# GpSimd subtractions and residual steps issued as four 256-column quarters, residual steps issued behind the first feed-forward products, and one engine per PSUM bank for scaling transposed blocks

## The chip, the cores and the metric

The kernel runs on one core of a Trainium2 chip. The metric is device time in microseconds (us). The engines are named as in the profile: PE is TensorE's matmul, PEld its weight load, DVE is VectorE, ACT is ScalarE, POOL is GpSimd, SP is SyncE, which here only issues transfers. SBUF is the memory on the chip that the engines work in, PSUM the eight banks that PE writes.

## The reference

Four residual layers of two blocks work on 256 tokens of width 1024, in float32. What matters here is the first block:

```python
for layer in range(2):                     # layer 0: latent attention, layer 1: state space mixer
    for mixer in (attention_or_ssm, mlp):
        scale, shift, gate = split(silu(c) @ W_mod + b_mod, 3)
        y = mixer(x * (1 + scale) + shift)         # mlp: relu(h @ W1)**2 @ W2
        x = layer_norm(ALPHA * x + (1 + gate) * y) # with a gain g and a bias b
```

The second block follows it: two layers with gated feed-forwards of hidden width 2816 before and behind a gated linear recurrence ("lru") in one layer and a block-sparse attention in the other, with RMS normalisation.

## The kernel before

The 256 tokens are two halves of 128 partitions. Weights come from HBM as units of 128x1024 float32 (512 KB) into seven raw buffers, in the order of a list. Each unit is split into two fp32r parts: `wh` is a copy made on ACT (L454), `wl = raw - wh` a subtraction (L455) on DVE for 445 units and on POOL for the 39 units of a table called POOLED. Every product is then made in three passes (xh·wh, xh·wl, xl·wh). Units of the modulation weights are not split but reduced on DVE (L504). A queue of the next units runs beside the products: each product step emits what is needed to prepare units further on, and each engine works its own instructions in that order.

A layer ends, and the next begins, in `boundary()`. The last products of tokens half 0 come first. Their result is gated and added to the old x (`ln_part`: L643, L644), its mean and variance are taken (L645 to L649, with one power on POOL, L627), and R is normalised in place by two DVE instructions of 128x512 (L658). Then `turn_x` (L593) transposes the eight 128x128 blocks of R[half] into two PSUM banks of four blocks each, a few units before the last products of the other half are through. `make_xt` scales each transposed block with a factor and a shift per feature, which are columns, and splits the result into xh (ACT, L585) and xl (DVE, L586). In one bank, blocks 0 and 2 are scaled on DVE (L610) and blocks 1 and 3 on ACT (L608). Three boundaries have this scaling: behind the attention's output (called mla_o, at 144 to 190 us), behind the first feed-forward (mlp0.d, 396 to 430 us) and behind the state space mixer (ssm_out, 555 to 596 us). With half 0 turned, the first product of the next layer for half 0 runs, then the same for half 1.

At the three boundaries POOL also makes the new residual for the next layer, x = r*g + b, for both halves in two instructions of 128x1024 each (`ln_resid`, L661 and L662). They are issued at the end of `boundary()`, and the next layer's `f_evac` copies the first products of a feed-forward layer out of PSUM into the same tiles R that the residual is made from.

Of the kernel before, what the change touches and what calls it, by code (L numbers as in the profile page):

```python
# [15 lines left out]
OP = mybir.AluOpType  # L16
# [36 lines left out]
# ------------------------------------------------------------ the order in which weights come  # L53
# [67 lines left out]
# ------------------------------------------------------------------------- host side layout  # L121
# [192 lines left out]
# ------------------------------------------------------------------------------- the kernel  # L314
class Model:
# [54 lines left out]
    # ---- small helpers  # L370
# [29 lines left out]
    # ---- weights  # L400
# [22 lines left out]
    def run(self, look=LOOK, maxn=99, mods=2):  # L423
        n = 0
        while self.nproc < len(UNITS) and n < maxn:
            i = self.nproc
            u = UNITS[i]
            if WPOS[i] > WPOS[self.ntake] + look:
                break
            if u[0] == "m":  # L430
                if mods == 0 or (self.hold and self.modfin is not None):
                    break
                mods -= 1
            self._issue(i + 1)
            if self.ndma <= i:
                break
            raw = self.raw[RPOS[i] % RAWN]
            self.settle(KEEP)
            if u[0] == "w":
                while self.rt and self.nw % RING in SPARE:  # L440
                    self.nw += 1
                s = self.nw % RING
                own = self.slot_owner[s]
                if own is not None and own not in self.finished:
                    break
                if own is None and s >= RING - 3 and self.early:
                    break
                if self.Hs[s] is None:
                    self.Hs[s], self.Ls[s] = (self.sb.tile([128, 1024], F32R, name="w%s%d_%d" % (c, s, i), tag="w%s%d" % (c, s))
                                              for c in "hl")  # L450
                self.nw += 1
                self.slot_owner[s] = u
                self.slot_of[u] = s
                self.nc.scalar.activation(self.Hs[s], raw, func=AF.Copy)  # L454
                (self.nc.gpsimd if u[1:] in POOLED else self.nc.vector).tensor_tensor(  # L455
                    self.Ls[s], raw, self.f32(self.Hs[s]), op=OP.subtract)
            elif u[0] == "m":
                self.mod_unit(u, raw)
# [29 lines left out]
    # ---- modulation: silu(c) @ w + b  # L488
# [44 lines left out]
    # ---- one step of the tensor engine has been emitted: t is its time in us  # L533
# [16 lines left out]
    # ---- matrix products in three float32r passes  # L550
# [37 lines left out]
    # ---- token-major -> feature-major, with a factor (and a shift) per feature  # L588
# [7 lines left out]
    def xt_evac(self, b, half, g, f, s, sh, perm):  # L596
        nc = self.nc
        hs = slice(128 * half, 128 * half + 128)
        ks = slice(4 * g, 4 * g + 4)
        f3 = (b if s is None else f).rearrange("p (k t) -> p k t", k=4)  # L600
        if s is not None:
            for j in range(4):
                k = 4 * g + j
                o, i = f[:, 128 * j:128 * j + 128], b[:, 128 * j:128 * j + 128]
                if perm:
                    o, i = o.rearrange("p (j k) -> p k j", j=4), i.rearrange("p (k j) -> p k j", j=4)
                if j % 2:
                    nc.scalar.activation(o, i, func=AF.Identity, scale=s[:, k:k + 1], bias=sh[:, k:k + 1])  # L608
                else:
                    nc.vector.tensor_scalar(o, i, s[:, k:k + 1], sh[:, k:k + 1], op0=OP.mult, op1=OP.add)  # L610
        self.split(self.XH[:, ks, hs], self.XL[:, ks, hs], f3)
        self.rel(b)
# [4 lines left out]
    def make_xt(self, half, bs, s=None, sh=None, perm=False):  # L617
        for g in range(2):
            self.xt_evac(bs[g], half, g, self.Z[2][:, 512 * (2 * half + g):512 * (2 * half + g) + 512], s, sh, perm)

    # ---- normalisations, one half of the tokens at a time
# [38 lines left out]
    def ln_resid(self, half, eng):  # L660
        eng.tensor_tensor(self.X[half], self.R[half], self.GR, op=OP.mult)  # L661
        eng.tensor_tensor(self.X[half], self.X[half], self.BR, op=OP.add)  # L662

    # x / rms(x) * pre, from the sums of squares
# [33 lines left out]
    # ---- the end of one layer and the start of the next  # L698
# [66 lines left out]
    # ---- feed-forward layers  # L765
    def ffn(self, tag, nt, first, begin, b1=None, epi=None, mid=None):
# [8 lines left out]
        for m in range(first, nt, 2):  # L775
# [12 lines left out]
            if m == first:  # L788
                self.f_hidden(pair, b1)
                if tag == "mlp0":  # L790
                    self.bg, self.hold = self.ssm_operators(), True
                if accs is None:
                    accs = [[self.bank(), self.bank()] for h in range(2)]
# [29 lines left out]
    def f_evac(self, half, outs, pair):  # L823
        nc, R = self.nc, self.R[half]
# [19 lines left out]
    def f_hidden(self, pair, b1):  # L844
        for i in range(2 if pair else 4):
            b = self.pair_transposes(self.R, 2 * i)
# [25 lines left out]
    # ---- small accurate functions on narrow tiles  # L872
# [36 lines left out]
    # ---- start: constants, rotary tables, first modulation  # L909
# [84 lines left out]
    # ---- attention of one head over 256 tokens, causal  # L994
# [29 lines left out]
    # ---- latent attention  # L1024
    def mla(self):
# [121 lines left out]
        def norm(h):  # L1147
            if h == 1:
# [6 lines left out]
                             self.post_ln, "mlp0.f", kouter=True, gate="mod02")  # L1155
# [5 lines left out]
    # one head after another, its stages spread over the next ones (a digit is the lag in heads)  # L1161
# [54 lines left out]
    # ---- state space layer: operators from the parameters  # L1216
# [97 lines left out]
    # tables of rotations and rows of the input operators (powers times B)  # L1314
# [42 lines left out]
    def ssm_operators(self):  # L1357
# [7 lines left out]
        # output operators, and the part within a chunk  # L1365
# [116 lines left out]
    # ---- state space layer: 64 chunks of 4 tokens, two groups of channels at a time  # L1482
    def ssm(self, begin):
# [154 lines left out]
        for i in range(4):  # L1638
            t = self.Z[2][:, 512 * i:512 * i + 512]
            for j in range(2):  # L1640
# [15 lines left out]
                             self.post_ln, "mlp1.f", kouter=True, gate="mod22")  # L1656
# [17 lines left out]
    # ---- gated linear recurrence  # L1674
# [27 lines left out]
    def lru(self, begin):  # L1702
# [4 lines left out]
        self.f_evac(0, fa, False)  # L1707
        fb = self.f_pass(1, fu)
        self.f_evac(1, fb, False)
# [124 lines left out]
    # ---- keys and values, kept over one feed-forward layer  # L1834
# [25 lines left out]
    def moba(self, begin):  # L1860
        nc = self.nc
        fu, fa = begin
        self.f_evac(0, fa, False)
        fb = self.f_pass(1, fu)
        self.f_evac(1, fb, False)
# [26 lines left out]
    # ---- the whole  # L1892
# [113 lines left out]
```

## Time and profile before

| | |
|---|---|
| three runs | 1795.33, 1793.89, 1794.28 us, median 1794.28 |
| span of the profiled execution | 1790.9 us (its time outside the span is not listed; the median is 3.4 us above the span) |
| busy shares | PE 90%, PEld 79%, DVE 67%, ACT 47%, POOL 24% |
| mean granted TensorE clock | 0.95 of full speed |
| DMA | 349.6 MB, mean 195 GB/s |

PE is the busiest engine by far. What it doesn't work, some 180 us, is spread over many places, and each such place has its own wait. A busy share tells nothing of them; the list of PE's waits by releaser and the timeline around each place do.

### The profile page before, as it was taken

The page shows a single profiled execution, that of the slowest core. Times are in us where ns is not written, and L with a number is a line of the kernel's source. Part 1 is how long each engine was busy: PE and PEld are TensorE (multiplying, and loading weights), DVE is VectorE, ACT ScalarE, POOL GpSimd, SP SyncE. Part 2 cuts the span into 40 slices and gives each one's busy share as a digit, 9 for nine tenths or more (in the row PEclk, how much of TensorE's full clock was granted, in tenths as well). Part 3 has the DMA queues.
Part 4 walks back from the last instruction along what each step waited for, and adds up shares of the span by engine and source line. Part 5 has one row for each costly group of instructions (what it writes and reads, how often), then busy time and mean ns, then how long its engine had stood idle before and what let it go on. Part 6 is the DMA issues. An engine that isn't in the chain of part 4 may idle for free. (4 is left out here: it accounts for less than half of the span.)

```text
span 1790.9 us, 25130 instructions
## 1 busy us (share of the span) xinstructions
PE 1607.8 (90%) x9690; PEld 1417.8 (79%) x9690; DVE 1192.7 (67%) x1480; ACT 835.3 (47%) x1252; POOL 433.7 (24%) x404
## 2 busy tenths in 40 slices
PE   4777998898778999999999838999999999899998
PEld 2555798786676799879998827999899999779997
DVE  6688795567988755586556787555656554856553
ACT  2342645565334645444445545444445444744441
POOL 8943198714725200000002351000000001120000
PEclk9869999898798999999999969999999999999999
DMA  9476577775655466645553433656356564526640
GB/s 370 165 267 215 203 262 261 252 270 192 224 184 200 174 247 220 229 170 205 196 172 127 134 126 133 230 204 204 113 212 220 179 225 142 177 95 223 207 158 24
DMA packets 106587, 349.63 MB, mean 195 GB/s; under 512 B 12385, under 2 KB 22753, under 8 KB 106466
## 3 DMA queue, kind: packets, MB, share of 16 engines
q1 hardware_dynamic: 106466, 348.02, 55.3%
q8 instruction: 76, 1.25, 0.3%
q14 instruction: 45, 0.37, 0.1%
HBM read 338.40 MB, written 9.57 MB: 194 GB/s over the span
## 5 line engine op out<-in xcount | busy, mean ns | idle before, releaser
L455 DVE TENSOR_TENSOR wl<-raw,wh 128x1024 fp32r<-128x1024 f32 x445 | 567.9, 1310 | 191.2 <-ACT wh L454 188.9
L454 ACT ACTIVATE wh<-raw 128x1024 fp32r<-128x1024 f32 x484 | 490.1, 1051 | 268.6 <-PE bank L392 135.0
L392 PE MATMUL bank<-xh,wh 128*128 128x256 f32 x1728 | 490.4, 284 | 0.0
L392 PE MATMUL bank<-xh,wl 128*128 128x256 f32 x1728 | 489.6, 283 | 0.0
L392 PE MATMUL bank<-xl,wh 128*128 128x256 f32 x1728 | 489.1, 283 | 0.0
L392 PEld LDWEIGHTS bank<-xh,wh 128*128 128x128 f32 x1728 | 331.1, 192 | 2.6 <-DVE z L1560 0.2
L392 PEld LDWEIGHTS bank<-xl,wh 128*128 128x128 f32 x1728 | 331.0, 192 | 2.1
L392 PEld LDWEIGHTS bank<-xh,wl 128*128 128x128 f32 x1728 | 330.9, 191 | 0.0
L392 PE MATMUL bank<-wh,hh 128*128 128x512 f32 x736 | 294.9, 401 | 30.8 <-ACT hh L1812 27.1
L392 PE MATMUL bank<-wl,hh 128*128 128x512 f32 x736 | 292.1, 397 | 2.6 <-POOL wl L455 2.5
L392 PE MATMUL bank<-wh,hl 128*128 128x512 f32 x736 | 243.3, 396 | 6.8 <-DVE hl L586 4.9
L627 POOL TENSOR_TENSOR st<-st,mhalf 128x1 f32<-128x1 f32 (+1 forms) x33 | 21.9, 664 | 720.1 <-DVE st L635 623.7
L392 PEld LDWEIGHTS bank<-wh,hh 128*128 128x128 f32 x736 | 140.7, 191 | 62.3 <-ACT hh L1812 28.4
L392 PEld LDWEIGHTS bank<-wh,hl 128*128 128x128 f32 x736 | 139.9, 190 | 40.1 <-DVE hl L586 5.7
L392 PEld LDWEIGHTS bank<-wl,hh 128*128 128x128 f32 x736 | 140.8, 191 | 32.2 <-POOL wl L455 3.7
L455 POOL TENSOR_TENSOR wl<-raw,wh 128x1024 fp32r<-128x1024 f32 x39 | 106.5, 2745 | 184.1 <-ACT wh L454 183.4
L504 DVE SCALAR_TENSOR_TENSOR junk<-raw,cs 128x1024 bf16<-128x1024 f32 x96 | 137.5, 1433 | 18.0 <-DMA raw<-in_ws_dram 16.9
L392 PE MATMUL bank<-wh,xh 128*128 128x512 f32 x320 | 132.3, 413 | 6.0 <-ACT xh L585 5.3
L392 PE MATMUL bank<-wl,xh 128*128 128x512 f32 x320 | 130.7, 408 | 6.2 <-DVE wl L455 6.1
L586 DVE TENSOR_TENSOR hl<-z,hh 128x512 fp32r<-128x512 f32 x72 | 51.9, 721 | 96.8 <-ACT hh L585 96.8
L392 PE MATMUL bank<-wh,xl 128*128 128x512 f32 x320 | 104.4, 404 | 4.2 <-DVE xl L586 4.2
L585 ACT ACTIVATE hh<-z 128x512 fp32r<-128x512 f32 x72 | 45.5, 632 | 116.4 <-DVE z L860 104.5
(385 smaller groups left out, 1811.1 us busy)
## 6 DMA issues: line engine op xcount, KB each, us to landing
raw<-in_ws_dram SPq DMA_DIRECT2D x580, 512.0 KB
early<-in_ws_dram SPq DMA_DIRECT2D x10, 512.0 KB
grow<-in_rows_dram SPq DMA_DIRECT2D x9, 512.0 KB
brow<-in_rows_dram SPq DMA_DIRECT2D x6, 512.0 KB
ophh<-ops_d SPq DMA_DIRECT2D x6, 512.0 KB
ophl<-ops_d SPq DMA_DIRECT2D x6, 512.0 KB
gate<-in_rows_dram SPq DMA_DIRECT2D x5, 512.0 KB
tab_d<-early SPq DMA_DIRECT2D x4, 512.0 KB
```

Source lines behind the costliest of these rows:

```text
L392: self.nc.tensor.matmul(out, l, r, start=start, stop=stop)
L454: self.nc.scalar.activation(self.Hs[s], raw, func=AF.Copy)
L455: (self.nc.gpsimd if u[1:] in POOLED else self.nc.vector).tensor_tensor(self.Ls[s], raw, self.f32(self.Hs[s]), op=OP.subtract)
L504: nc.vector.scalar_tensor_tensor(self.junk, raw, 1.0, self.cs, op0=OP.mult, op1=OP.mult, accum_out=total)
L585: self.nc.scalar.activation(hdst, src, func=AF.Copy)
L586: self.nc.vector.tensor_tensor(ldst, src, self.f32(hdst), op=OP.subtract)
L627: self.nc.gpsimd.tensor_tensor(r, v, self.mhalf[:, 0:n], op=OP.pow)
```

## The change

There are three parts. First, a POOLED subtraction and each of the two residual steps is no longer one POOL instruction over 1024 columns but four over 256 columns; in the residual the multiply and the add of one quarter follow each other. Second, behind the attention and behind the state space mixer the residual is issued in `ffn()` behind `f_hidden` and no longer at the end of `boundary()`, and `f_evac` of these feed-forwards writes to a scratch tile (Z[0]) and not to R. Third, `make_xt` scales all four blocks of the first bank on ACT and all four of the second on DVE, and only then splits both banks.

```diff
-                (self.nc.gpsimd if u[1:] in POOLED else self.nc.vector).tensor_tensor(
-                    self.Ls[s], raw, self.f32(self.Hs[s]), op=OP.subtract)
+                if u[1:] in POOLED:
+                    for q in range(4):
+                        w = slice(256 * q, 256 * q + 256)
+                        self.nc.gpsimd.tensor_tensor(self.Ls[s][:, w], raw[:, w], self.f32(self.Hs[s])[:, w], op=OP.subtract)
+                else:
+                    self.nc.vector.tensor_tensor(self.Ls[s], raw, self.f32(self.Hs[s]), op=OP.subtract)
...
-    def xt_evac(self, b, half, g, f, s, sh, perm):
...
-                if j % 2:
+                if g:
+                    nc.vector.tensor_scalar(o, i, s[:, k:k + 1], sh[:, k:k + 1], op0=OP.mult, op1=OP.add)
+                else:
                     nc.scalar.activation(o, i, func=AF.Identity, scale=s[:, k:k + 1], bias=sh[:, k:k + 1])
-                else:
-                    nc.vector.tensor_scalar(o, i, s[:, k:k + 1], sh[:, k:k + 1], op0=OP.mult, op1=OP.add)
-        self.split(self.XH[:, ks, hs], self.XL[:, ks, hs], f3)
-        self.rel(b)
...
         for g in range(2):
-            self.xt_evac(bs[g], half, g, self.Z[2][:, 512 * (2 * half + g):512 * (2 * half + g) + 512], s, sh, perm)
...
+            self.xt_split(bs[g], half, g, fs[g])
...
     def ln_resid(self, half, eng):
-        eng.tensor_tensor(self.X[half], self.R[half], self.GR, op=OP.mult)
-        eng.tensor_tensor(self.X[half], self.X[half], self.BR, op=OP.add)
...
+        for q in range(4):
+            w = slice(256 * q, 256 * q + 256)
+            eng.tensor_tensor(self.X[half][:, w], self.R[half][:, w], self.GR[:, w], op=OP.mult)
+            eng.tensor_tensor(self.X[half][:, w], self.X[half][:, w], self.BR[:, w], op=OP.add)
...
             if m == first:
                 self.f_hidden(pair, b1)
+                if not pair:
+                    self.post_ln()
...
-    def f_evac(self, half, outs, pair):
-        nc, R = self.nc, self.R[half]
+    def scratch(self, r):
+        return self.R if r else [self.Z[0][:, 1024 * h:1024 * h + 1024] for h in range(2)]
+
+    def f_evac(self, half, outs, pair, lru=False):
+        nc, R = self.nc, self.scratch(pair or lru)[half]
...
-                             self.post_ln, "mlp0.f", kouter=True, gate="mod02")
+                             None, "mlp0.f", kouter=True, gate="mod02")
...
-                             self.post_ln, "mlp1.f", kouter=True, gate="mod22")
+                             None, "mlp1.f", kouter=True, gate="mod22")
```

VectorE at mla_o, tokens half 0, from its five modulation units' last to the next `ln_part`; `z` is the scaled block, `bank_126` and `bank_128` are the two transposed banks. Before:

```order
L504 SCALAR_TENSOR_TENSOR junk,msum<-raw_64,cs 128x1024 [waits DMAHW6_49,DVE_49]
L610 TENSOR_SCALAR z_100<-bank_126,scol,bcol 128x128 [waits PE_49]
L610 TENSOR_SCALAR z_100<-bank_126,scol,bcol 128x128 [waits Activation_49]
L586 TENSOR_TENSOR xl<-z_100,xh 128x4x128 [waits DVE_49,Activation_49]
L610 TENSOR_SCALAR z_100<-bank_128,scol,bcol 128x128 [waits PE_49]
L610 TENSOR_SCALAR z_100<-bank_128,scol,bcol 128x128 [waits Activation_49]
L586 TENSOR_TENSOR xl<-z_100,xh 128x4x128 [waits DVE_49,Activation_49]
L643 TENSOR_TENSOR r_93<-bank_131,gate 128x512 [waits PE_49]
```

And of the change, at the same place:

```order
L508 SCALAR_TENSOR_TENSOR junk,msum<-raw_64,cs 128x1024 [waits DMAHW6_49,DVE_49]
L623 TENSOR_SCALAR z_100<-bank_128,scol,bcol 128x128 [waits PE_49]
L623 TENSOR_SCALAR z_100<-bank_128,scol,bcol 128x128 x3
L590 TENSOR_TENSOR xl<-z_100,xh 128x4x128 [waits Activation_49] x2
L651 TENSOR_TENSOR r_93<-bank_131,gate 128x512 [waits PE_49]
```

DVE's second scaling of each bank no longer waits for ACT, and both `xl` stand behind all scaling.

GpSimd at the same boundary, from the power of half 1 (L627) to the state space layer's operators (L1362), which it makes next. Before:

```order
L627 TENSOR_TENSOR st<-st,mhalf 128x1 [waits DVE_49]
L455 TENSOR_TENSOR wl_54_839<-raw_69,wh_54_838 128x1024 [waits DMAHW3_49,DMAHW6_49,PE_49,Activation_49]
L661 TENSOR_TENSOR x_90<-r_92,grow 128x1024 [waits DMAHW0_49]
L662 TENSOR_TENSOR x_90<-x_90,brow 128x1024 [waits DMAHW1_49,Pool_49]
L661 TENSOR_TENSOR x_91<-r_93,grow 128x1024 [waits DVE_49]
L662 TENSOR_TENSOR x_91<-x_91,brow 128x1024 [waits Pool_49]
L1362 TENSOR_TENSOR r_92<-z_99,spp 128x4x5x16 [waits DMAHW4_49,PE_49,Activation_49]
```

And of the change, from the same power on, with the residual of half 0 to its fourth quarter:

```order
L635 TENSOR_TENSOR st<-st,mhalf 128x1 [waits DVE_49]
L458 TENSOR_TENSOR wl_54_839<-raw_69,wh_54_838 128x256 [waits DMAHW3_49,DMAHW6_49,PE_49,Activation_49]
L458 TENSOR_TENSOR wl_54_839<-raw_69,wh_54_838 128x256
L458 TENSOR_TENSOR wl_54_839<-raw_69,wh_54_838 128x256 [waits PE_49]
L458 TENSOR_TENSOR wl_54_839<-raw_69,wh_54_838 128x256
L671 TENSOR_TENSOR x_90<-r_92,grow 128x256 [waits DMAHW0_49]
L672 TENSOR_TENSOR x_90<-x_90,brow 128x256 [waits DMAHW1_49,Pool_49]
L671 TENSOR_TENSOR x_90<-r_92,grow 128x256
L672 TENSOR_TENSOR x_90<-x_90,brow 128x256 [waits Pool_49]
L671 TENSOR_TENSOR x_90<-r_92,grow 128x256
L672 TENSOR_TENSOR x_90<-x_90,brow 128x256 [waits Pool_49]
L671 TENSOR_TENSOR x_90<-r_92,grow 128x256
```

On GpSimd the residual keeps its place in the queue, behind the same weight unit and ahead of the same operators; only its pieces are smaller, and each add waits for the multiply just ahead of it.

ScalarE behind the first products of half 0 at the same boundary, where the results are copied out of PSUM. The first fence is of before, the second of the change; each begins with the last two copies into `xh`, or the one ahead of it, and the scaling of half 1.

```order
L608 ACTIVATE z_100<-bank_127,bcol,scol 128x128 [waits DVE_49] x2
L585 ACTIVATE xh<-z_100 128x4x128 [waits Activation_49]
L608 ACTIVATE z_100<-bank_129,bcol,scol 128x128 [waits DVE_49] x2
L585 ACTIVATE xh<-z_100 128x4x128 [waits Activation_49]
L832 ACTIVATE r_92<-bank_124 128x512 [waits PE_49,Pool_49]
```

```order
L625 ACTIVATE z_100<-bank_127,bcol,scol 128x128 [waits PE_49]
L625 ACTIVATE z_100<-bank_127,bcol,scol 128x128 x3
L589 ACTIVATE xh<-z_100 128x4x128 [waits Activation_49]
L589 ACTIVATE xh<-z_100 128x4x128 [waits DVE_49]
L847 ACTIVATE z_98<-bank_124 128x512 [waits PE_49]
```

ACT's scaling waits for the transposes alone and no longer for DVE's scaling of a neighbouring block, its second `xh` waits for DVE's four blocks, and the copy out of PSUM no longer waits for POOL.

## Rows read from the trace of the kernel before

**Rows 1.** Head of the page: span, busy time and share of each engine.

```profile
span 1790.9 us, 25130 instructions
PE 1607.8 (90%) x9690; PEld 1417.8 (79%) x9690; DVE 1192.7 (67%) x1480; ACT 835.3 (47%) x1252; POOL 433.7 (24%) x404
```

**Rows 2.** PE's waits, 144 to 190 us: total, times, longest, us.

```profile
PE bank L593 <- DVE r L658: 7.6, 4, 3.6
PE bank L392 <- ACT xh L585: 3.9, 1, 3.9
PE bank L392 <- DVE wl L455: 1.8, 1, 1.8
```

**Rows 3.** PE's waits, 396 to 430 us.

```profile
PE bank L593 <- DVE r L658: 3.0, 2, 1.6
PE bank L392 <- DVE wl L455: 1.8, 2, 1.4
PE bank L392 <- ACT xh L585: 1.4, 1, 1.4
```

**Rows 4.** PE's waits, 555 to 596 us.

```profile
PE bank L593 <- DVE r L658: 7.7, 4, 3.2
```

**Rows 5.** Timeline, mla_o, GpSimd and VectorE: start, duration, instruction, idle before.

```profile
148.90 4.87 POOL L455 TENSOR_TENSOR wl<-raw,wh 128x1024 fp32r<-128x1024 f32 x2
148.97 5.08 DVE L658 TENSOR_SCALAR r<-r,st 128x512 f32<-128x512 f32 x2 [0.68 <-POOL st L627]
...
167.19 2.63 DVE L644 SCALAR_TENSOR_TENSOR r<-x,r 128x512 f32<-128x512 f32 x1
...
173.70 5.04 DVE L658 TENSOR_SCALAR r<-r,st 128x512 f32<-128x512 f32 x2 [0.68 <-POOL st L627]
178.66 3.37 DVE L455 TENSOR_TENSOR wl<-raw,wh 128x1024 fp32r<-128x1024 f32 x1
```

**Rows 6.** Timeline, mlp0.d, VectorE, half 0.

```profile
398.05 1.00 DVE L658 TENSOR_SCALAR r<-r,st 128x512 f32<-128x512 f32 x2 [0.67 <-POOL st L627]
```

**Rows 7.** Timeline around 242 and 260 us, POOL working on 256 columns.

```profile
241.88 1.90 DVE L455 TENSOR_TENSOR wl<-raw,wh 128x1024 fp32r<-128x1024 f32 x1
242.66 1.71 POOL L1362 TENSOR_TENSOR gate<-brow 128x256 f32<-128x256 f32 x1
...
260.57 0.73 POOL L1362 TENSOR_TENSOR gate<-brow 128x256 f32<-128x256 f32 x1
```

**Rows 8.** Timeline, mla_o, half 0, VectorE: first scaling, second, last split.

```profile
160.19 0.41 DVE L610 TENSOR_SCALAR z<-bank,scol,bcol 128x128 f32<-128x128 f32 x1
161.12 0.41 DVE L610 TENSOR_SCALAR z<-bank,scol,bcol 128x128 f32<-128x128 f32 x1 [0.53 <-ACT z L608]
...
165.86 0.69 DVE L586 TENSOR_TENSOR xl<-z,xh 128x512 fp32r<-128x512 f32 x1 [1.19 <-ACT xh L585]
```

**Rows 9.** Groups of POOL instructions by line: count, busy us, mean ns.

```profile
L455 POOL TENSOR_TENSOR wl<-raw,wh 128x1024 fp32r<-128x1024 f32 x39 | 106.5, 2745 | 184.1 <-ACT wh L454 183.4 <-DVE z L1672 0.6
```

**Rows 10.** Timeline, state space layer, POOL: a chain of three weight units.

```profile
463.93 9.86 POOL L455 TENSOR_TENSOR wl<-raw,wh 128x1024 fp32r<-128x1024 f32 x3
```

**Rows 11.** PE's waits, 430 to 555 us.

```profile
PE bank L392 <- POOL z L1574: 7.7, 2, 4.4
PE bank L392 <- POOL wl L455: 2.5, 2, 1.9
```

**Rows 12.** PE's waits, 950 to 1160 us.

```profile
PE bank L392 <- ACT hh L1812: 27.1, 2, 26.7
PE bank L593 <- DVE r L669: 3.1, 2, 1.8
```

**Rows 13.** PE's waits, 1490 to 1620 us.

```profile
PE bank L392 <- DVE xl L586: 4.2, 1, 4.2
```

**Rows 14.** Busy time by stretch: PE, PEld, DVE, ACT, POOL, granted clock, DMA share, GB/s.

```profile
144.00:190.00 46.00, 32.78 (x127) 25.20 (x126) 37.23 (x43) 11.47 (x18) 21.28 (x10) 0.85 0.46 169
190.00:390.00 200.00, 182.85 (x1163) 164.85 (x1163) 140.17 (x136) 123.82 (x201) 122.33 (x97) 0.97 0.77 266
```

More of the change, by code (lines that the diff above doesn't have):

```diff
@@ L594, in transposes, with xt_split @@
         return b
-    def xt_evac(self, b, half, g, f, s, sh, perm):
-        nc = self.nc
+    def xt_split(self, b, half, g, f):
         hs = slice(128 * half, 128 * half + 128)
         ks = slice(4 * g, 4 * g + 4)
[L600 to L606, printed above, removed]
-                if j % 2:
-                    nc.scalar.activation(o, i, func=AF.Identity, scale=s[:, k:k + 1], bias=sh[:, k:k + 1])
-                else:
-                    nc.vector.tensor_scalar(o, i, s[:, k:k + 1], sh[:, k:k + 1], op0=OP.mult, op1=OP.add)
-        self.split(self.XH[:, ks, hs], self.XL[:, ks, hs], f3)
+        self.split(self.XH[:, ks, hs], self.XL[:, ks, hs], f.rearrange("p (k t) -> p k t", k=4))
         self.rel(b)
@@ L617, in make_xt @@
     def make_xt(self, half, bs, s=None, sh=None, perm=False):
+        nc = self.nc
+        if s is None:
+            for g in range(2):
+                self.xt_split(bs[g], half, g, bs[g])
+            return
+        fs = [self.Z[2][:, 512 * (2 * half + g):512 * (2 * half + g) + 512] for g in range(2)]
+        for j in range(4):
+            for g in range(2):
+                k = 4 * g + j
+                o, i = fs[g][:, 128 * j:128 * j + 128], bs[g][:, 128 * j:128 * j + 128]
+                if perm:
+                    o, i = o.rearrange("p (j k) -> p k j", j=4), i.rearrange("p (k j) -> p k j", j=4)
+                if g:
+                    nc.vector.tensor_scalar(o, i, s[:, k:k + 1], sh[:, k:k + 1], op0=OP.mult, op1=OP.add)
+                else:
+                    nc.scalar.activation(o, i, func=AF.Identity, scale=s[:, k:k + 1], bias=sh[:, k:k + 1])
         for g in range(2):
-            self.xt_evac(bs[g], half, g, self.Z[2][:, 512 * (2 * half + g):512 * (2 * half + g) + 512], s, sh, perm)
+            self.xt_split(bs[g], half, g, fs[g])
     def rpow(self, v, n=1):
@@ L845, in f_hidden @@
         for i in range(2 if pair else 4):
-            b = self.pair_transposes(self.R, 2 * i)
+            b = self.pair_transposes(self.scratch(pair), 2 * i)
             hh = self.HH[:, 2 * i:2 * i + 2, :].rearrange("p a t -> p (a t)")
@@ L1706, in lru @@
         fu, fa = begin
-        self.f_evac(0, fa, False)
+        self.f_evac(0, fa, False, True)
         fb = self.f_pass(1, fu)
-        self.f_evac(1, fb, False)
+        self.f_evac(1, fb, False, True)
         sp2, br, bi = (self.col(n, 0, 8) for n in ("lam", "lbr", "lbi"))
@@ L1862, in moba @@
         fu, fa = begin
-        self.f_evac(0, fa, False)
+        self.f_evac(0, fa, False, True)
         fb = self.f_pass(1, fu)
-        self.f_evac(1, fb, False)
+        self.f_evac(1, fb, False, True)
         Q = [(self.GATE, self.GR)[h // 4][:, 256 * (h % 4):256 * (h % 4) + 256] for h in range(8)]
```

## The prediction

> **What bounds the kernel now.** I read the head of the page first: PE is busy 90% of the span and nothing else comes near [rows 1]. So time can only come from PE's idle time, some 183 us, or from its clock; work taken off another engine is worth nothing by itself. The list of PE's waits was next, one stretch at a time. At the three boundaries with scaling, PE waits for the normalisation (L658), for xh and for wl: 13.3 us at mla_o [rows 2], 6.2 at mlp0.d [rows 3], 7.7 at ssm_out [rows 4]. All of these releasers are on DVE or wait for DVE. So I read DVE's timeline there. A pair of normalising instructions takes 1.00 us while POOL is idle [rows 6] and 5.08 us while POOL works on two weight units, and both end together: POOL's two from 148.90 to 153.77, DVE's from 148.97 to 154.05 [rows 5]. Five of the six pairs show this 5 us, the sixth is the one in rows 6. The same holds for L644 (2.63 us) and wl (3.37 us) in rows 5. The reading is that a DVE instruction with this kind of SBUF operands and a POOL instruction take turns, each waiting for the whole of the other. At 256 columns the turns are short: a DVE wl there took 1.90 us, and a POOL instruction of that width 1.71 us, against 0.73 us alone [rows 7].
>
> **Part 1, quarters.** A DVE instruction that meets POOL will wait for at most one quarter, about 0.73 us [rows 7], and not for a unit of 2.44 us (4.87 / 2, [rows 5]). The change removes no POOL work. Where POOL is alone, four quarters cost 4 × 0.73 = 2.9 us against 2.44, so each unit and each residual step comes some 0.5 us later; where DVE is full of such instructions, a unit takes up to 4 × 1.71 = 6.8 us. The cover for this is that POOL is idle 76% of the span [rows 1] and that PE needs most of these units later. The Trainium skill advises against small tiles (Advanced Engine Details and Errata, The Read-Write Bubble: a gap between instructions makes tiles of 512 or 1024 elements better), but says that GpSimd has no such gap. By that page quartering would cost POOL nothing; the POOL rows here show the 0.5 us above, and the sum goes by those.
>
> At mla_o, half 0's normalisation would shrink from 5.08 to at most 1.00 + 2 × 0.73 = 2.5 us, but five modulation reductions stand behind it on DVE, which meet the remaining quarters instead, so half 0's scaling starts no earlier (I take 0.4 us later). For half 1, L644 goes from 2.63 to about 0.69 + 0.73 = 1.4 (0.69 is the free time of a two-operand instruction of that size, [rows 8]), a gain of 1.2; L658 from 5.04 to 2.5, a gain of 2.5; wl from 3.37 to 1.90, a gain of 1.5 [rows 5, 7].
>
> **Part 2, residuals behind the first products.** The order of POOL's queue is the same before and after, since nothing else stands between. Neither does the copy out of PSUM gain: ACT's wait for POOL falls away, but POOL had finished with that half. I cost it at 0. It protects: with quarters the residual may end later than before, and PE's path no longer depends on it. Without it, a residual of 16 instructions of up to 1.71 us would end up to 27 us after it began.
>
> **Part 3, one engine per bank.** In rows 8 DVE waits 0.53 us for ACT's block between two blocks of its own, then 1.19 us for xh; half 0 takes from 160.19 to 166.55, 6.4 us. With four blocks of 0.41 on DVE and two splits of 0.69, and ACT's bank finished beforehand (its transposes are there early, since DVE is the late one), DVE needs 3.0 us. That is a gain of 3.4, less the 0.4 of part 1: 3.0. ACT now gets its first bank without DVE. What can be lost is that its second xh waits for DVE's four blocks with weight copies queued behind it; ACT is 47% busy [rows 1], so 0.
>
> **The sum.** At mla_o the half 1 path gains 3.0 + 1.2 + 2.5 + 1.5 = 8.2 us, and part 3 again for half 1 adds about 1: 9, out of the 13.3 that PE waits there [rows 2]. At the other two boundaries the same steps work on smaller waits. PE can't get more than it waits; from 6.2 [rows 3] I take 5 (the xh wait of 1.4 and the wl waits go, half of L658's 3.0 is the floor of a free pair and a quarter), from 7.7 [rows 4] 6. Bounds of each: 0 if turns stay as long as they are, and the whole wait.
>
> A second gain is the clock. In 144 to 190 us PE was granted 0.85 of full speed, while in the following stretch with less idle time it got 0.97 [rows 14]. PE is busy some 33 us in the first of these; at 0.97 that would be 33 × (1 − 0.85 / 0.97) = 4 us less. Three such stretches have at most 12 us; I take 3, since the waits don't all go.
>
> In the state space stage (430 to 555 us) quarters work both ways: DVE's work there gets through POOL's chains of three units sooner, but the chain, 9.86 us now [rows 10], lies between 12 × 0.73 = 8.8 and 12 × 1.71 = 20.5 us, and POOL's own L1574, for which PE waits 7.7 us, stands behind one [rows 11]. I take 0, from −6 to +5. In the second block, L669's 3.1 us [rows 12] and xl's 4.2 us [rows 13] are again DVE caught by POOL: I take 4 of these 7.3. What is gained in the recurrence ahead of L1812 is mostly lost in the 27 us wait there [rows 12], whose chain runs on DVE, ACT and POOL.
>
> Behind each boundary stands a long stretch with PE near full, the first with transfers at 0.77 of the engines' time [rows 14], so an earlier start carries through to the end as long as weights keep up. Sum: 9 + 5 + 6 + 3 + 0 + 4 = 27 us off the span of 1790.9 [rows 1], so 1764; with the 3.4 us by which the median of the runs stands above that span, about 1767.
>
> **The rivals.** The forecast's mechanism, short turns, I hold at 0.58, for 1757 to 1776.
>
> Gain given back downstream, 0.18: the first stretch behind mla_o already moves 266 GB/s [rows 14], and POOL in it works 122 of 200 us on the operators of the state space layer. If weights or those operators set its end, the 9 of mla_o come back as waits, with what the clock gave: 1794 − 15 = 1779, range 1776 to 1787. Against it: PE has only 17 us of idle time in that stretch, so it is PE that sets its end.
>
> More than that, 0.10: all waits of the three sites (27 us), 8 of the clock, 5 of the state space stage and 7 of the second block go, 47 us: 1747, and everything from there to 1757 counts here.
>
> No change, 0.06: turns are not one for one, and POOL, whose next quarter stands ready, issues all four before DVE gets its turn. Then a DVE instruction waits 2.9 us and nothing shortens; part 3 alone remains, 2 × 1 to 3 us, most of it behind waits of L658: 1790 to 1797. Against it, the 1.90 us of wl among ready POOL instructions [rows 7]. The Trainium skill (SBUF — State Buffer, SBUF: two separate sides) says that the shared ports go for a whole instruction to whichever engine starts first; it doesn't say who is first when both stand ready, which is this rival's question.
>
> Slower, 0.08: the quarters make POOL the late engine. The mechanism's place is the chains of three units, five of them in the program, two of these in the state space stage. At 20.5 us in place of 9.9, each brings its last unit, and what POOL does behind it, 10.6 us later. PE already waits 2.5 us for POOL's wl and 7.7 for L1574 [rows 11], so there is no slack in two of the five. If four of five put 10.6 us on PE, 42 us are lost against 27 gained: 1809. It decides from about 7 us a chain. For it: units are 2745 ns in the mean already [rows 9], that is, they meet DVE. Against it: DVE is busy 67% of the time [rows 1] and has work against POOL for only part of a chain.
>
> **How the numbers follow.** The forecast is 1767 us. The range of 1752 to 1786 leaves out the slower case, the part of the no-change case above it, and the lower end of the case of more gain, together under 0.2; the forecast's own range stands with it. A change under 0.2% (3.6 us) can hardly be told from none. Faster 0.86, same 0.06, slower 0.08.
>
> **What would show it.** Right: L658's pairs at the three boundaries at 1.7 to 2.6 us in place of 5; L644 and wl at 1.4 and 1.9; POOL's quarters at 0.7 alone and up to 1.7 against DVE; DVE's scaling of half 0 at mla_o through in about 3 us; PE's waits for L658 down from 18 us over the whole run to under 7; the granted clock in the three stretches above 0.85. Part 2 would be right if POOL's residual ends later than before and PE or ACT don't wait for it. Wrong: L658 still at 5 us (no short turns); PE's waits for POOL's wl, for L1574 or for ACT's hh growing by what the boundaries gave; or PE idle time between 190 and 390 us well above 17 us.

## The result and the profile after

The changed kernel takes 1743.87 us (median of four runs, 1742.75 to 1746.06) against 1794.24 us of the kernel before on the same chip: a ratio of 0.972 with a 95% interval of 0.9704 to 0.9736. It is faster by 50 us, where 27 were forecast and 42 was the edge of the range. The profiled run took 1742.75 us with a span of 1740.9.

The head of the page of the changed kernel, to be read against [rows 1]:

```profile
span 1740.9 us, 25278 instructions
PE 1602.5 (92%) x9690; PEld 1417.2 (81%) x9690; DVE 1157.7 (67%) x1480; ACT 833.7 (48%) x1252; POOL 508.8 (29%) x557
```

PE's work is nearly the same, POOL's busy time has grown by 75 us, and DVE's has shrunk by 35 us, although DVE works the same 1480 instructions on the same data. What DVE lost is time in which it was held up.

PE issues the same 9690 matmuls in the same order in both kernels. So a stretch of the program can be cut at the same matmul in both, and its two lengths compared. Here are the three boundaries, cut that way, in the kernel before (stretch, length, PE busy and its matmuls, PEld, DVE, ACT, POOL, granted clock, DMA share, GB/s):

```profile
144.00:205.00 61.00, 46.90 (x213) 37.64 (x212) 51.94 (x59) 22.42 (x30) 21.28 (x10) 0.89 0.53 191
396.00:430.00 34.00, 27.84 (x109) 21.25 (x108) 24.39 (x33) 11.29 (x18) 13.30 (x6) 0.85 0.42 155
555.00:600.00 45.00, 37.25 (x148) 29.65 (x147) 36.22 (x38) 17.13 (x25) 26.54 (x12) 0.85 0.40 138
```

And the same matmuls in the changed kernel:

```profile
142.87:190.76 47.89, 43.42 (x213) 36.38 (x212) 44.69 (x56) 22.43 (x30) 38.79 (x33) 0.93 0.71 242
381.06:404.21 23.15, 23.09 (x109) 18.71 (x108) 19.94 (x33) 11.28 (x20) 11.65 (x12) 1.00 0.50 182
527.55:560.80 33.25, 32.47 (x148) 26.09 (x147) 28.24 (x38) 17.50 (x25) 31.07 (x36) 1.00 0.59 210
```

The boundaries became 13.1, 10.9 and 11.8 us shorter. In the second line PE is busy for 23.09 of 23.15 us, at the full clock: there the limit is now PE itself, and no shorter wait can gain more. PE's idle time fell by 9.6, 6.1 and 7.0 us, and its busy time by 3.5, 4.8 and 4.8 us, for the same matmuls at a higher clock.

The mechanism that the prediction named is in the timeline of the changed kernel. DVE at mla_o, half 1 (compare [rows 5]), then the pair at mlp0.d that meets nothing and the one that meets the residual (compare [rows 6]):

```profile
166.68 1.83 DVE L666 TENSOR_SCALAR r<-r,st 128x512 f32<-128x512 f32 x2 [0.67 <-POOL st L635]
168.43 1.76 DVE L460 TENSOR_TENSOR wl<-raw,wh 128x1024 fp32r<-128x1024 f32 x1
...
383.12 1.00 DVE L666 TENSOR_SCALAR r<-r,st 128x512 f32<-128x512 f32 x2 [0.67 <-POOL st L635]
...
394.23 1.83 DVE L666 TENSOR_SCALAR r<-r,st 128x512 f32<-128x512 f32 x2 [0.44 <-POOL st L635]
```

The five long pairs went from 5.04 to 5.08 us down to 1.82 to 1.84, below the bound of 2.5; wl went from 3.37 to 1.76, and the 2.63 us of L644 became 0.95 (L652). PE's waits for the normalisation, 18.3 us in all before, are 0.8 us. What was new is on POOL's side. At mla_o the residual of both halves now takes from 170.74 to 193.88 us, 23 us for 16 quarters:

```profile
170.74 0.74 POOL L671 TENSOR_TENSOR x<-r,grow 128x256 f32<-128x256 f32 x1
...
175.22 9.62 DVE L460 TENSOR_TENSOR wl<-raw,wh 128x1024 fp32r<-128x1024 f32 x6
...
192.30 1.58 POOL L672 TENSOR_TENSOR x<-x,brow 128x256 f32<-128x256 f32 x1
...
195.62 1.57 PE L856 MATMUL bank<-ident,z 128*128 128x128 f32 x7 [4.20 <-DVE z L848]
```

In that time six wl on DVE take 9.62 us, 1.6 each. DVE's copy of half 1 out of PSUM (L848) stands behind them, and PE waits 4.2 us for it. This is most of the 4.6 us that the next stretch gives back. The same stands behind ssm_out: PE waits 2.2 us for L848 there, a wait that the kernel before does not have, and the stretch gives back 3.0 us.

### The profile page after: what moved, and what is told of

It is laid out like the page before. It is cut to its first block, busy times and chain, and to the rows that moved or that the text cites. A ratio compares the mean times of both kernels' runs of the same rounds, so it can differ in the third digit from the quotient of the medians.

```text
span 1740.9 us, 25278 instructions
## 1 busy us (share of the span) xinstructions
PE 1602.5 (92%) x9690; PEld 1417.2 (81%) x9690; DVE 1157.7 (67%) x1480; ACT 833.7 (48%) x1252; POOL 508.8 (29%) x557
## 5 line engine op out<-in xcount | busy, mean ns | idle before, releaser
L458 POOL TENSOR_TENSOR wl<-raw,wh 128x256 fp32r<-128x256 f32 x156 | 156.7, 1037 | 138.0 <-ACT wh L454 129.8
L508 DVE SCALAR_TENSOR_TENSOR junk<-raw,cs 128x1024 bf16<-128x1024 f32 x96 | 138.0, 1437 | 18.3 <-DMA raw<-in_ws_dram 17.1
L392 PE MATMUL bank<-wl,xh 128*128 128x512 f32 x320 | 126.6, 396 | 1.9 <-DVE wl L460 1.0
L392 PE MATMUL bank<-wh,xh 128*128 128x512 f32 x320 | 127.4, 398 | 0.7 <-ACT wh L454 0.7
```

Source lines behind the costliest of these rows:

```text
L392: self.nc.tensor.matmul(out, l, r, start=start, stop=stop)
L458: self.nc.gpsimd.tensor_tensor(self.Ls[s][:, w], raw[:, w], self.f32(self.Hs[s])[:, w], op=OP.subtract)
L508: nc.vector.scalar_tensor_tensor(self.junk, raw, 1.0, self.cs, op0=OP.mult, op1=OP.mult, accum_out=total)
```

## The experiments

All times are medians, each against the kernel before run beside it (1793.4 to 1794.5 us). The table shows by how many us the same matmuls came sooner (−) or later (+) in each stretch; it is worked out from the starts of the matmuls in the traces. Columns: the changed kernel; quarters alone; banks alone; weight quarters with parts 2 and 3; residual quarters with parts 2 and 3; halves; eighths; the changed kernel without weight steps on POOL; the kernel before without weight steps on POOL. Of the stretches left out, 0 to 144 us differs by −1.3 to +1.7 us among these kernels, the others by 0.1.

```
stretch (before)    chg  quart  banks   wl-q  res-q  halves 8ths  noPOOL before-noPOOL
144-205 mla_o     -13.1   -8.9   -4.0   -9.3   -9.9   -9.0 -15.6  -13.6   -4.0
205-280            +4.6   +4.0   -0.2   +0.7   +3.4   +1.1  +1.2   +1.7   +0.9
280-396            -5.3   -3.0   +1.7   -1.6   -4.9   -2.8  -1.1   -1.6   -2.1
396-430 mlp0.d    -10.9   -3.5   -5.7   -5.6  -10.9   -8.7 -11.3  -10.9    0.0
430-555            -1.7   -1.6   -0.2   -1.7   +1.7   -3.0 +15.2   -7.8   -9.0
555-600 ssm_out   -11.8  -10.2   -4.6   -8.5   -6.2   -9.0  -9.4  -11.1   -1.5
600-960            +3.0   +1.6   +0.1   +1.2   +0.1   +1.6  +1.8   +1.2   +0.3
960-1110           -7.9   -8.0   -2.7   -7.4   -0.5   -6.6  -4.9  -12.5  -11.9
1520-1605          -5.8   -6.1   -0.2   -4.7   -0.2   -0.3  -4.8   -5.8   -4.8
```

### Which part carries the gain

Quarters alone: the residual back at the boundary's end, R as target of the copy, scaling alternating.

```diff
-        for j in range(4):
-            for g in range(2):
+        for g in range(2):
+            for j in range(4):
...
-                if g:
+                if j % 2:
...
-                if not pair:
-                    self.post_ln()
...
-        return self.R if r else [self.Z[0][:, 1024 * h:1024 * h + 1024] for h in range(2)]
+        return self.R if True else [self.Z[0][:, 1024 * h:1024 * h + 1024] for h in range(2)]
...
-                             None, "mlp0.f", kouter=True, gate="mod02")
+                             self.post_ln, "mlp0.f", kouter=True, gate="mod02")
...
```

> Only part 1: weight and residual steps in quarters on GpSimd; the residual stays at the end of the boundary, the copy out of PSUM goes to R, and the scaling alternates as before. Theory A (short turns between GpSimd and VectorE carry the gain, and TensorE's clock follows from the shorter waits): most of the 50 us, 1750 to 1765 us, the normalising pairs at 2.5 us or less. Rival B (the scaling by one engine per bank carries it, by 3 us at each of six scalings and the clock behind them): 1775 to 1794. Rival C (quarters pay only if the residual is out of the way of the copy out of PSUM, which then waits for 16 short instructions): 1775 or more, with ScalarE's copy waiting for GpSimd at two places.

1759.66 us, ratio 0.9812 (0.9793 to 0.9831): 34 of the 50 us, as theory A says; rival C falls.

Banks alone: part 1 and part 2 undone.

```diff
-                    for q in range(4):
-                        w = slice(256 * q, 256 * q + 256)
-                        self.nc.gpsimd.tensor_tensor(self.Ls[s][:, w], raw[:, w], self.f32(self.Hs[s])[:, w], op=OP.subtract)
+                    self.nc.gpsimd.tensor_tensor(self.Ls[s], raw, self.f32(self.Hs[s]), op=OP.subtract)
...
```

> Only part 3: one engine per bank scales; GpSimd works on whole tiles as before. Theory A: a few us, 1784 to 1792, since the path still goes through normalising pairs of 5 us. Rival B: 1750 to 1770.

1778.87 us, 0.9923 (0.9901 to 0.9945): 14 us, more than theory A's 2 to 10 and less than rival B's. They stand at the three boundaries, some 4 to 6 us at each, also where the normalising pair still takes 5 us. Another 2.7 us stand in 960 to 1110 us, where no block is scaled; no run tells why.

Part 2 alone (whole tiles, alternating scaling, residual behind `f_hidden`, copy into the scratch tile):

> Only part 2: residual behind the first products and the copy out of PSUM into a scratch tile. Theory A and rival B: no change, 1791 to 1797, since the copy did not wait for GpSimd before. Rival C, in its form that the move itself is worth something: under 1788.

1792.90 us, 0.9995 (0.9985 to 1.0005): nothing, as forecast.

Parts 2 and 3, whole tiles on POOL:

> Parts 2 and 3 without part 1: GpSimd on whole tiles. Theory A: as part 3 alone, 1784 to 1792. Rival B: 1750 to 1765. If neither part nor their pair gives 50 us and quarters alone do not either, the parts work only together, which neither theory says.

1777.15 us, 0.9913 (0.9897 to 0.993): between the two expectations again, and as banks alone. In the total the parts add up: 34 for quarters and 14 for banks make 48 of the 50 us. By place they do so only roughly: at mlp0.d the two kernels' gains make 9.2 us against 10.9 together, at ssm_out 14.8 against 11.8.

### Which quarters, and how small

Weight quarters with a whole residual, then residual quarters with whole weight steps (parts 2 and 3 in both):

```diff
-        for q in range(4):
-            w = slice(256 * q, 256 * q + 256)
-            eng.tensor_tensor(self.X[half][:, w], self.R[half][:, w], self.GR[:, w], op=OP.mult)
...
+        eng.tensor_tensor(self.X[half], self.R[half], self.GR, op=OP.mult)
...
```

> The changed kernel with the residual steps whole again (two instructions of 1024 columns a half); weight steps stay in quarters. No quarters at all gave 1777, both kinds 1744. Theory A (what counts is the longest GpSimd instruction that VectorE meets on the path): the residual meets the second half's path at two boundaries, mla_o and mlp0.d and ssm_out's second normalisation, so 1755 to 1765, with pairs of 5 us only where the residual stands beside them. Rival D (weight steps carry nearly all): 1744 to 1750. Rival E (residual steps carry nearly all): 1770 to 1778.

> The changed kernel with the weight steps whole again; residual steps stay in quarters. Theory A: about as much again, 1757 to 1768, and none of the gains behind 960 us, which has no residual steps on GpSimd. Rival D: 1770 to 1778. Rival E: 1744 to 1752.

1754.89 us, 0.9792 (0.9772 to 0.9813), and 1765.15 us, 0.9845 (0.9823 to 0.9868). Both count; neither rival D nor E holds. Theory A was right on the place too: residual quarters do all that can be done at mlp0.d, where no weight unit stands, and nothing behind 960 us; weight quarters bring the 12 us there. The mean normalising instruction, as the groups by line show it, is 1430 ns in the first and 1563 in the second, between 2231 and 886.

Halves of 512 columns in place of quarters (`range(2)`, 512):

> The changed kernel with halves of 512 columns in place of quarters. Theory A: the turn is 1.2 to 1.3 us and not 0.73, so between whole tiles (1777) and quarters (1744), 1750 to 1760. Rival F (turns are not one for one, quarters help in another way): as quarters, 1744, or as whole tiles, 1777.

1755.38 us, 0.9793 (0.9772 to 0.9813): between whole tiles and quarters, as theory A says. Eighths of 128 columns (`range(8)`, 128):

> The changed kernel with eighths of 128 columns. Theory A: turns get shorter by less (0.73 to perhaps 0.45 us) while GpSimd pays more instructions: 1738 to 1748. If what counts is the number of turns and not their length (each costs VectorE a fixed time): 1750 or more.

1763.19 us, 0.982 (0.9805 to 0.9835): slower than theory A allows, and in the range of a fixed price for each turn. By place it splits. At mla_o eighths beat quarters by some 2.4 us, but in the state space stage they lose 15.2 us against the kernel before. The last group of runs looks for that loss.

The turns themselves did what theory A says. Here are the same two DVE instructions, the pair of half 1 at mlp0.d, with the POOL instructions beside them: whole tiles (the kernel before), halves, quarters (the changed kernel, whose pair of 1.83 us at 394.23 stands above) and eighths.

```profile
412.73 2.36 POOL L661 TENSOR_TENSOR x<-r,grow 128x1024 f32<-128x1024 f32 x1
415.17 2.41 POOL L662 TENSOR_TENSOR x<-x,brow 128x1024 f32<-128x1024 f32 x1
412.80 5.07 DVE L658 TENSOR_SCALAR r<-r,st 128x512 f32<-128x512 f32 x2 [0.44 <-POOL st L627]
...
397.94 1.29 POOL L671 TENSOR_TENSOR x<-r,grow 128x512 f32<-128x512 f32 x1
399.30 1.36 POOL L672 TENSOR_TENSOR x<-x,brow 128x512 f32<-128x512 f32 x1
398.00 2.95 DVE L666 TENSOR_SCALAR r<-r,st 128x512 f32<-128x512 f32 x2 [0.44 <-POOL st L635]
...
394.17 0.73 POOL L671 TENSOR_TENSOR x<-r,grow 128x256 f32<-128x256 f32 x1
394.98 0.80 POOL L672 TENSOR_TENSOR x<-x,brow 128x256 f32<-128x256 f32 x1
...
394.49 0.46 POOL L671 TENSOR_TENSOR x<-r,grow 128x128 f32<-128x128 f32 x1
395.03 0.52 POOL L672 TENSOR_TENSOR x<-x,brow 128x128 f32<-128x128 f32 x1
394.56 1.28 DVE L666 TENSOR_SCALAR r<-r,st 128x512 f32<-128x512 f32 x2 [0.45 <-POOL st L635]
```

At all four sizes the pair lasts as long as its two POOL instructions and 0.30 us more: 5.07, 2.95, 1.83 and 1.28 us. With both residual and weight steps on DVE the pair takes 1.00 us at every boundary. So the two engines alternate, and the length of POOL's instruction sets the price of a turn; a fixed price for each turn is out.

### Is the clock a gain of its own?

The kernel before, with transposes of the identity ahead of the transposes for which PE waits:

```diff
+BUSY = {("mla_o", 0): (5, 8), ("mla_o", 1): (20, 6), ("mlp0.d", 1): (9, 6), ("ssm_out", 0): (18, 6), ("ssm_out", 1): (8, 8)}
...
+        for j in range(fill):
+            self.nc.tensor.transpose(b[:, 0:128], self.ident, self.ident)
...
```

> The kernel before, with 94 extra transposes of the identity, which no result uses, ahead of the transposes for which TensorE waits at the three boundaries; they fill some 3/4 of each of these waits and add no other work. Theory A's second half (in the three stretches 13 us of the gain are busy TensorE time that became shorter, because the granted clock did not fall): the clock in these stretches is granted higher than 0.85 to 0.89 and the run takes 1783 to 1790. If the clock follows something else than TensorE's idle time: 1793 to 1800, the clock as before.

1795.42 us, 1.0008 (0.9993 to 1.0023): no gain, and yet the clock rose. The three boundaries of this kernel, cut at the same matmuls, with the extra transposes in them (columns as above):

```profile
142.39:203.14 60.75, 50.07 (x252) 40.97 (x251) 51.80 (x59) 22.42 (x30) 21.31 (x10) 0.94 0.53 194
394.19:427.66 33.47, 26.64 (x124) 19.93 (x122) 23.83 (x32) 10.72 (x17) 13.33 (x6) 1.00 0.42 157
553.26:597.99 44.73, 37.51 (x188) 30.39 (x187) 35.97 (x38) 16.87 (x24) 26.56 (x12) 1.00 0.39 136
```

At mlp0.d and ssm_out the clock went from 0.85 to 1.00, at mla_o from 0.89 to 0.94. The stretches became 0.3, 0.5 and 0.3 us shorter. So the lower clock cost next to nothing in the kernel before: PE had time to work slowly, because DVE's chain set the length of these stretches. The second half of theory A is refuted for this kernel. Two other runs agree: with whole tiles and one engine per bank, mlp0.d takes 28.2 us at a clock of 0.94 (banks alone) and 28.2 us at 1.00 (parts 2 and 3).

With a short chain it is another matter. In the changed kernel PE is busy all but 0.06 us at mlp0.d. Had the same matmuls stayed busy for the 27.84 us of the kernel before, the stretch could have become 6.2 us shorter and not 10.9, by this estimate. So the clock adds nothing while the chain is long, and the full gain needs both. No run held the clock down beside a short chain.

### Is GpSimd's help worth having?

The changed kernel with all weight steps on VectorE:

```diff
-POOLED = {('att_o', 4), ('att_o', 6), ...}
+POOLED = set()
```

> The changed kernel with no weight step on GpSimd: all 484 on VectorE, residual quarters stay on GpSimd. Theory G (a weight unit on GpSimd costs VectorE up to four turns of 0.73 us, 2.9 us, where VectorE would do it in 1.2 us, so GpSimd's help costs more than it takes wherever VectorE is full of two-operand work): 1730 to 1744. Rival H (GpSimd works mostly while VectorE is idle or reads PSUM, so its help is cheap): 47 us more VectorE work, part of it on the path, 1750 to 1770.

1734.76 us, 0.9667 (0.965 to 0.9683): faster than the changed kernel by 9 us, as theory G says. By the table, 6.1 us of this stand in 430 to 555 us and 4.6 in 960 to 1110 us. The groups by line show DVE's weight steps of this kernel:

```profile
L460 DVE TENSOR_TENSOR wl<-raw,wh 128x1024 fp32r<-128x1024 f32 x484 | 598.5, 1273 | 192.4 <-ACT wh L454 190.5
```

and its page the totals:

```profile
PE 1586.1 (92%) x9690; PEld 1405.6 (81%) x9690; DVE 1169.9 (68%) x1519; ACT 832.9 (48%) x1252; POOL 359.7 (21%) x401
```

39 more weight steps at some 1.2 us would be 47 us of DVE time; DVE's busy time grew by 12.2 (1157.7 to 1169.9). The other 35 us, 0.9 for each step, are by this difference what POOL's quarters had held DVE up.

The residual on VectorE, whole, and then both on VectorE:

```diff
-            self.ln_resid(h, self.nc.gpsimd)
+            self.ln_resid(h, self.nc.vector)
```

> The changed kernel with the residual steps on VectorE, whole, at the same places in the program; weight quarters stay on GpSimd. Theory G: VectorE pays 4.9 us a boundary itself in place of 16 turns of 0.73 us (11.7), so the 4.6 us that the changed kernel gives back behind mla_o and the 2.8 behind ssm_out shrink: 1736 to 1744. Rival H: VectorE is the late engine just there, 1745 to 1755.

> Both moved to VectorE: GpSimd does neither weight nor residual steps. Theory G: the two gains together, 1725 to 1740. Rival H: the two losses together, 1755 to 1780.

1746.36 us, 0.9731 (0.9713 to 0.9749), and 1734.15 us, 0.9663 (0.9647 to 0.9679). The first lies 1.4 us inside rival H's range, the second in theory G's. For the residual neither side wins: within the intervals both equal the same kernel with the residual in quarters on GpSimd. Theory G holds for weight steps, not for the residual, whose 16 quarters cost about what VectorE's own four instructions do.

Then the kernel before with nothing changed but `POOLED = set()`:

> The kernel before with all 484 weight steps on VectorE and nothing else changed. The quarters of the weight steps were worth some 21 to 33 us (1777 or 1765 against 1744). If that was harm avoided that GpSimd's whole tiles did to VectorE (theory G), taking them off GpSimd is worth at least as much here: 1755 to 1765. If whole tiles on GpSimd were a net help before and only their length on the boundaries' path hurt (rival H): 1775 to 1795.

1762.16 us, 0.9825 (0.9803 to 0.9846), as theory G says. With 39 more weight steps to work, DVE is busy for 17.7 us less than the 1192.7 of [rows 1]:

```profile
PE 1600.2 (91%) x9690; PEld 1413.6 (80%) x9690; DVE 1175.0 (67%) x1519; ACT 835.2 (47%) x1252; POOL 332.7 (19%) x365
```

Taking the weight steps off POOL gives as much as quartering everything on it (1759.66), in other places: 21 of the 32 us come in 430 to 555 and 960 to 1110 us, and mlp0.d, where the residual alone stands, gets nothing.

Without weight steps on POOL, the residual whole, and in eighths:

> No weight step on GpSimd, residual steps there whole. Residual quarters were worth 11 us beside weight quarters (1755 against 1744). If that is the half 1 path at the three boundaries: 1742 to 1748 here against 1735. If the residual only hurt together with weight units ahead of it in GpSimd's queue: 1733 to 1738.

> No weight step on GpSimd, residual steps there in eighths of 128 columns. Eighths gave the best times at mla_o and mlp0.d (15.6 and 11.3 us against 13.1 and 10.9 of quarters) and lost 15 us in the state space stage, where GpSimd's chains of three weight units stand. Theory: without weight units that loss can't arise, 1730 to 1735. If eighths of the residual alone make GpSimd late for the state space layer's operators: 1740 or more.

Whole: 1746.52 us, 0.9737 (0.9721 to 0.9753), so the residual's quarters are worth 11.8 us by themselves, in the range for the half 1 path. Eighths: 1741.47 us, 0.9707 (0.9691 to 0.9723), slower than quarters by 6.7 us. The theory that eighths lose by POOL's chains of weight units is refuted as the whole story, since this kernel has none. Its timeline in the state space stage:

```profile
430.06 1.23 DVE L508 SCALAR_TENSOR_TENSOR junk<-raw,cs 128x1024 bf16<-128x1024 f32 x1 [10.23 <-DMA raw<-in_ws_dram]
...
432.07 0.66 PE L392 MATMUL bank<-z,oph 128*128 128x64 f32 x2 [11.08 <-DVE z L1545]
```

and the waits of its SP queue from 380 to 440 us, then the same wait with quarters (the kernel without weight steps on POOL):

```profile
SPq L1528 <- POOL x L671: 19.4, 1, 19.4
```

```profile
SPq L1528 <- POOL x L671: 8.3, 2, 8.1
```

L1528 loads a table into the tile from which POOL's residual multiplies (the row g), so it waits in SP's queue until POOL's last multiply. With eighths the residual of mlp0.d takes 25 us on POOL and not 15, the queue stands for 19.4 us, weight transfers stand behind it, DVE waits 10.23 us for one, and PE 11.08 us for DVE. This is read from the trace; no run moved the table's load. In the kernel with eighths everywhere the same queue waits 16.4 us, and PE waits 8.9 us for the same instruction of DVE and 11.1 us for POOL's L1589, so that both causes may be at work there.

## Why the prediction was wrong

**What bounds, right.** POOL and DVE take turns, and a turn's length is that of POOL's instruction. What was worked out from [rows 5 to 7] came out or was beaten: a pair 1.83 us against 2.5, wl 1.76 against 1.90, L644 0.95 against 1.4, and 1.00 for the pair that meets nothing. The no-change rival, in which POOL issues all its quarters before DVE's turn, would have given pairs of at least four quarters, 2.9 us.

**The cap on two boundaries, wrong: the step that failed.** The sum said "PE can't get more than it waits" and took 5 us of 6.2 [rows 3] and 6 of 7.7 [rows 4]. They gave 10.9 and 11.8. PE's idle time did about what the sum said: at the three boundaries it fell by 9.6, 6.1 and 7.0 us, against 9, 5 and 6. What the cap left out is that PE's busy time can fall as well; it fell by 13.1 us in all, and the sum had 3 for it. The length of these stretches was set not by PE but by DVE's chain. Its ends in the kernel before, at mla_o and ssm_out, from the first gating to the last split:

```profile
143.66 0.69 DVE L643 TENSOR_TENSOR r<-bank,gate 128x512 f32<-128x512 f32 x1 [1.02 <-PE bank L392]
...
181.95 0.40 DVE L610 TENSOR_SCALAR z<-bank,scol,bcol 128x128 f32<-128x128 f32 x1
...
189.72 0.69 DVE L586 TENSOR_TENSOR xl<-z,xh 128x512 fp32r<-128x512 f32 x1 [1.19 <-ACT xh L585]
...
555.78 0.69 DVE L643 TENSOR_TENSOR r<-bank,gate 128x512 f32<-128x512 f32 x1
...
595.68 0.69 DVE L586 TENSOR_TENSOR xl<-z,xh 128x512 fp32r<-128x512 f32 x1 [1.19 <-ACT xh L585]
```

and in the changed kernel:

```profile
142.53 0.69 DVE L651 TENSOR_TENSOR r<-bank,gate 128x512 f32<-128x512 f32 x1 [1.02 <-PE bank L392]
...
170.96 1.37 DVE L623 TENSOR_SCALAR z<-bank,scol,bcol 128x128 f32<-128x128 f32 x4 [0.77 <-PE bank L597]
172.72 1.97 DVE L590 TENSOR_TENSOR xl<-z,xh 128x512 fp32r<-128x512 f32 x2 [0.40 <-ACT xh L589]
...
528.23 0.69 DVE L651 TENSOR_TENSOR r<-bank,gate 128x512 f32<-128x512 f32 x1 [1.94 <-PE bank L392]
...
553.13 1.82 DVE L590 TENSOR_TENSOR xl<-z,xh 128x512 fp32r<-128x512 f32 x2
```

The chains went from 46.8 to 32.2 us and from 40.6 to 26.7, 14.6 and 13.9 us shorter, and the stretches by 13.1 and 11.8. PE's own wait before was less than this because PE worked at a lower clock inside the chain, which looks like work in the busy share. The run with extra transposes shows that this was slack. The prediction added up the chain's shortenings for mla_o and left this off for the other two. An estimate of that sum, with its own prices (2.5 for a pair, 1.90 for wl, 1.4 for L644, 3.0 to 3.4 for a scaling, 0.7 more where its last split meets a quarter), gives 10 to 11 us at mlp0.d and 15 at ssm_out: right at the first, some 3 too many at the second, and nearer than 5 and 6 at both.

**The clock, mis-sized and wrong in kind.** 3 us were added as a second gain. PE's busy time fell by 13.1 us in the three stretches, but a like rise of the clock without a shorter chain brought nothing. It is the other side of the chain's gain and a condition for all of it at mlp0.d, not a term beside it.

**Part 3, mis-sized.** It stands in the sum with some 4 us, all at mla_o; banks alone gave 14 us, as 4.0, 5.7 and 4.6 at the three boundaries. With two scalings at each boundary, that is between one and two times the 3.0 us worked out for a scaling. The 3.0 us was used for one boundary of three; at the other two it was lost under the cap. For half 1 at mla_o the sum has about 1; there the lines above show the scaling at 8.5 us before (181.95 to 190.41) and 3.7 after (170.96 to 174.69).

**mla_o, right in size by two errors.** 9 us were forecast. The stretch gave 13.1, and the next gave 4.6 back, as the residual's quarters held up DVE's weight steps for 23 us. The rival of a gain given back downstream was thus real in part, by way of DVE's queue and not of the weights or the operators that it named. The prediction said that the residual would end later and that nothing would wait for it. Nothing waits for the residual itself, but DVE's queue pays for it.

**The second block, mis-sized.** 4 us were forecast, 13.7 came (960 to 1110 and 1520 to 1605 us), 12 of them also with weight quarters and whole residual steps. PE's wait ahead of the recurrence's L1812 in [rows 12] did not swallow the gain: it fell by 3.3 us itself, since its chain has DVE in it too: six DVE instructions there (L1747, from 1014.29 us) took 7.2 us beside POOL's whole weight units and 5.4 in the changed kernel. A wait that [rows 12] leaves out, for DVE's copy out of PSUM, fell from 4.1 to 0.5 us. The first line is of before, in the window of [rows 12]; the second is of the changed kernel, from 923 to 1160 us:

```profile
PE bank L841 <- DVE r L833: 4.1, 1, 4.1
...
PE bank L392 <- ACT hh L1827: 23.8, 2, 23.4
```

**The state space stage and the slower rival.** 0 was taken, −1.7 was measured. The rival's chain of three units, 9.86 us in [rows 10], became 14.9 us, near the middle between the bounds of 8.8 and 20.5:

```profile
437.54 14.91 POOL L458 TENSOR_TENSOR wl<-raw,wh 128x256 fp32r<-128x256 f32 x12
```

PE's waits for POOL there grew mainly at one place (for L1589's ophh, from 3.7 to 7.8 us) and shrank at others. The rival was real in kind: with eighths the stage lost 15 us.

**The range.** The case of all waits going held 0.10 and stood at 1747, 3 us from the result. That nearness is in part luck: its sum takes 8 us for the clock, 5 for the state space stage, 7 for the second block and nothing given back, where 13.1, 1.7, 13.7 and a loss of 7.6 behind mla_o and ssm_out were measured. The range ended at 1752 because the caps were taken for bounds.

Open stays the stretch of 280 to 396 us, which differs by −5.3 to +1.7 us among kernels that change little in it. In the traces 5.0 of the 5.3 us are one wait of PE for one copy on DVE (L1461, L1476 in the changed kernel): 8.4 us before, 3.5 after. What makes it longer or shorter no run settles.

Together: of the 23 us that the sum lacked, some 13 stand at the three boundaries, 10 in the second block and 7 in the state space stage and 280 to 396 us; 8 were given back behind mla_o and ssm_out, and 1 stands ahead of 144 us.

## What to carry to other kernels

Where two engines take turns by whole instructions, the size of the helper's instruction is the price that the busy engine pays on its path; cut it, or ask whether the help is worth a turn at all: here the fastest kernel gives POOL no weight step (1734.76 us, the same within the intervals with the residual on DVE too). Size a gain by the chain that sets a stretch's length, not by the waits of the engine at its end, which may have spent the rest of the time working slowly. Smaller pieces have an end: at 128 columns the helper was late for a transfer queue.

## What the runs showed of the hardware

A pair of DVE instructions that met POOL lasted as long as two POOL instructions and 0.30 us more, at four sizes of POOL's instruction. As one instruction of 1024 columns, a weight step on POOL cost DVE more than a step of its own: with 39 more of them on DVE, the kernel before had DVE busy for 17.7 us less. In quarters it cost less than that, 0.9 us a step against 1.2, and the kernel was still faster without it, by 9 us. A rise of TensorE's granted clock from 0.85 to 1.00 in two stretches, made with useless transposes in its waits, changed their lengths by 0.5 and 0.3 us, while DVE set them.
